# One part of a depthwise convolution as matmuls with diagonal weights on TensorE

## Chip, cores and metric

The kernel runs on one core of one Trainium2 chip. The metric is the device time of one execution in microseconds (us), as the median of several runs.

## What is computed

One block of a hybrid network: x is 1024 tokens by 1024 channels. After a modulated RMS norm the input is projected (`w_in`) for two branches: a gated depthwise convolution of 512 channels with 31 taps, and an RWKV-7 recurrence of eight heads of 64 channels. Both are joined, projected (`w_out`) and added; a second modulated norm and a gated feed-forward network with a 3-tap convolution follow. The change touches the first branch alone:

```python
def causal_dwconv(x, w, b):
    K, C = w.shape
    y = lax.conv_general_dilated(x, w[:, None, :].astype(x.dtype), window_strides=(1,),
                                 padding=[(K - 1, 0)], dimension_numbers=('NWC', 'WIO', 'NWC'),
                                 feature_group_count=C)
    return y + b

def token_mix(h, w_in, conv_dw_w, conv_dw_b, ...):
    p = h @ w_in
    p_conv, p_rw = p[..., :2 * CONV_WIDTH], p[..., 2 * CONV_WIDTH:]
    u, u_gate = jnp.split(p_conv, 2, axis=-1)
    u = u * jax.nn.sigmoid(u_gate)
    u = causal_dwconv(u, conv_dw_w, conv_dw_b)
    u = jax.nn.silu((layer_norm(u, LN_EPS) * conv_ln_g + conv_ln_b).astype(h.dtype))
    ...
    return jnp.concatenate([u, y], axis=-1) @ w_out
```

## The kernel before

Everything lies channels by tokens: 128 channels on the partitions, 512 tokens (a **half**) along them; half 0 is tokens 0 to 511. The recurrence goes in four **units** of 256 tokens, 0 and 1 in half 0, 2 and 3 in half 1.

Matmuls of the projections keep nearly full precision with three products: each weight tile of 128x512 (four blocks of 128x128) is loaded by SP's queue, cast to a high part `wh` by ScalarE (L140) and reduced to a low part `wl` by GpSimd (POOL, L142); the inputs are split the same way. L158 multiplies `wh` by the high input, L159 `wh` by the low one, L160 `wl` by the high one, all into one PSUM bank.

Names: `p_r10` is the projection of r for half 1 and the first group of heads, `p_k11` that of k for the second group, `p_ug1_0` and `p_u1_0` the gate and the value of the convolution's part 0 of half 1. A unit has pair blocks (`s`, L621, split by VectorE (DVE) at L623 to L625), an inverse of a triangular matrix on DVE (`inverse`, L663 to L683) whose input `ab` and output `dd` pass through DRAM, a merge (`pt`, L701) and a chain of steps (`ch`, `y`). `bo` (L609) is a unit's bonus term, a full-precision 128x512 matmul of r with a constant; `bo20` and `bo21` are those of unit 2. `cm0` (L427) is the matmul that takes the mean over the channels of half 0's convolution, `o000` the first tile of the output projection of half 0, `up00` the first tile of its up-projection; `hl_o00` to `hl_o03` are the low parts of o's first inputs (L454), the convolution's results.

The convolution of a half (`conv`) has four parts of 128 channels. Parts 0 to 2 run on DVE (`vector`, L396): 31 operations each, a tap at a time, into a PSUM bank. Part 3 (`scalar`) runs on ScalarE, one multiplication a tap (L400, L403), and POOL, which adds each product to the sum (L404). The function is a generator: every `shifted` (a projection of half 1 mixed with its shifted self), `glu` and `up_tile` takes one step of it, `next(filler[0], None)`. For half 0 a step is eight DVE taps, with a tap of part 3 beside every third:

```python
while n < 3 * KC:
    for j in range(taps):
        i = next(v, None)
        ...
        if n % 3 == 0:
            i = next(s, None)
            ...
        n += 1
    yield
```

So half 0's convolution is strewn over half 1's input projections. The Tile scheduler orders the instructions of each engine by priorities; blocks under `first()` (recurrence, `conv_norm`, the splits of the convolution's results) and under `high_priority` (the output projection) come ahead of others once ready, and `keep_in_program_order` pins the first tap of a step.

Of the kernel before, what the change touches and what calls it, by code (L numbers as in the profile page):

```python
# [7 lines left out]
F32 = mybir.dt.float32  # L8
# [59 lines left out]
def build(nc, tc, I, O):  # L68
# [306 lines left out]
    def conv(half, accs, taps):  # L375
# [12 lines left out]

        def vector():

            for ct in range(3):
                u, acc = load(ct), bank(f"cv{half}_{ct}", "v")
                yield V.tensor_scalar(acc, u[:, 0:HT], cw(ct, 0), col("conv_b", ct), ALU.mult, ALU.add)
                for k in range(1, KC):
                    o = accs[ct] if k == KC - 1 else acc
                    yield V.scalar_tensor_tensor(o, u[:, k:k + HT], cw(ct, k), acc, ALU.mult, ALU.add)  # L396

        def scalar():
            u, acc = load(3), accs[3]
            yield S.activation(acc, u[:, 0:HT], AF.Identity, scale=cw(3, 0), bias=col("conv_b", 3))  # L400
            for k in range(1, KC):
                t = slot(cv, "ctmp", f"{half}_{k}", bufs=2)
                i = S.activation(t, u[:, k:k + HT], AF.Identity, scale=cw(3, k), bias=ZERO)  # L403
                G.tensor_tensor(acc, acc, t, ALU.add)  # L404
                yield i

        v, s = vector(), scalar()
        n = 0
# [12 lines left out]
    def conv_norm(accs, half, b):  # L421
# [7 lines left out]
        for ct in range(4):  # L429
            V.tensor_tensor(accs[ct], accs[ct], mean, ALU.add)  # L430
            sq = s2 if ct == 0 else slot(cv, "ctmp", f"sq{half}_{ct}", bufs=2)
            S.activation(sq, accs[ct], AF.Square, bias=ZERO)
            if ct:
                G.tensor_tensor(s2, s2, sq, ALU.add)
        rb = bcast(rstd(s2, f"cv{half}", ones, 1, 1.0 / CW, EPS_LN, tag="c", b=b), f"cv{half}", 1, b=b)
        for ct in range(4):
            V.tensor_tensor(accs[ct], accs[ct], rb, ALU.mult)
            t = slot(cv, "ctmp", f"th{half}_{ct}", bufs=2)
            S.activation(t, accs[ct], AF.Tanh, scale=col("ln_g", ct), bias=col("ln_b", ct))
# [67 lines left out]
    def v_tiles(half):  # L507

        new = lambda q, g: rw.tile([P, 2, QT], F32, name=f"v{2 * half + q}{g}", tag="v", bufs=5)
        t = {(q, g): new(q, g) for q, g in ((0, 0), (0, 1), (1, 0), (1, 1))}  # L510
# [26 lines left out]
    def group_back(q, g):  # L537
        kvr = []
        for x in range(3):
            t = rw.tile([P, 2, QT], F32, name=f"{'kvr'[x]}{q}{g}", tag="kvr"[x], bufs=(3, 5, 3)[x])  # L540
            nc.sync.dma_start(t, kvd[g][x][:, q % 2])
            kvr.append({q % 2: t})
# [481 lines left out]
    def unit(q, kvrs, la, before=None):  # L1024
# [4 lines left out]
        if before:  # L1029
            with first():  # L1030
# [8 lines left out]
    ctags = ("ctmp", "cu", "ctmp", "cu3", "cacc0")  # L1039
    spare = ada_rest(range(3), lambda i, n: slot(cv, ctags[i % 5], n, 30 + HT if ctags[i % 5][:2] == "cu" else HT,  # L1040
                                                 2 if ctags[i % 5] == "ctmp" else 1)[:, :HT],
# [95 lines left out]
def layout(inp):  # L1137
# [21 lines left out]
    for p in range(4):  # L1159
        cols += [12 + p, 16 + p, 8 + p]  # L1160
    win = mt(w_in[:, :22 * P])[cols]
    winl = w_in[:, 22 * P:].reshape(8, P, 1, 32).transpose(1, 0, 2, 3).repeat(3, 2).reshape(P, 768)
    ada = a["ada_w"][0]
    am = ada.reshape(8, P, 6, 2, HT).transpose(2, 3, 0, 1, 4)
# [25 lines left out]
```

## Time and profile before

| | us |
|---|---|
| median of 3 runs (1476.76 to 1481.39) | 1479.4 |
| the profiled execution | 1478.2 |
| its span, first to last instruction | 1476.4 |
| mean granted TensorE clock, share of full speed | 0.964 |

The profile is of one execution. TensorE is PE, its weight loads PEld, VectorE DVE, ScalarE ACT, GpSimd POOL, SyncE SP. A clock of 1.00 in a window is the higher of TensorE's two levels (2.4 GHz); below that, it spent part of the window at 1.2 GHz. Half 0's convolution lies between 235 and 379 us, the recurrence of unit 2 between 390 and 515, half 0's output projection between 460 and 553, and the first up-projection starts at 584.7 us.

### The profile page before, as it was taken

How to read it: one execution, taken by the hardware profiler on the slowest of the kernel's cores; microseconds unless marked ns; L12 is line 12 of the kernel's file. 1: busy time of each engine (PE TensorE's matmuls, PEld its weight loads, DVE VectorE, ACT ScalarE, POOL GpSimd, SP SyncE). 2: the span in 40 equal slices, each digit the busy share in tenths (PEclk: the TensorE clock that was granted, in tenths of full speed). 3: DMA queues.
4: the chain of work that ended last, by engine and by line, in shares of the span. 5: the costliest groups of instructions: out<-in, count | busy, mean ns of one | idle time of the engine just before them, and what ended most of it. 6: DMA issues, size and time to landing. Idle time of an engine off the chain costs nothing.

```text
span 1476.4 us, 23402 instructions
## 1 busy us (share of the span) xinstructions
PE 1379.4 (93%) x8412; PEld 1115.5 (76%) x8412; DVE 915.0 (62%) x1427; ACT 682.0 (46%) x1234; POOL 783.0 (53%) x716
## 2 busy tenths in 40 slices
PE   3999989999899997999999999999998999999995
PEld 2787867777577885777788787777887888888884
DVE  7667669899765466888779965562027555551102
ACT  5445354365553465444555454644233444443221
POOL 2545654588653354555666654457446555454443
PEclk9999989999899896999999999999999999999997
DMA  9394572345323753235337345883335323233332
GB/s 358 118 351 139 171 202 93 116 121 152 97 79 106 184 161 106 66 90 150 96 107 217 122 147 188 295 285 91 94 96 183 110 94 99 95 98 93 92 98 75
DMA packets 168484, 208.02 MB, mean 141 GB/s; under 512 B 64112, under 2 KB 79088, under 8 KB 168368
## 3 DMA queue, kind: packets, MB, share of 16 engines
q1 hardware_dynamic: 167792, 205.48, 44.5%
q8 instruction: 66, 1.08, 0.3%
q10 hardware_dynamic: 576, 1.05, 0.2%
q14 instruction: 50, 0.41, 0.1%
HBM read 172.39 MB, written 34.08 MB: 140 GB/s over the span
## 4 chain that ended last, share of the span: by engine, by line
PE 67%; DVE 18%; DMA 6%; issue 3%; ACT 2%; SPq 2%; POOL 1%; DVEq 0%; POOLq 0%; ACTq 0%
PE up L158 9%; PE up L159 9%; PE up L160 9%; PE d L160 5%; PE d L158 5%; PE d L159 5%; DVE cv L396 2%; PE o L160 1%; PE o L158 1%; PE o L159 1%; DVE rkp L599 1%; DVE bk L601 1%; DVE t_dx L678 1%; PE s L621 1%; PE hn L708 1%
## 5 line engine op out<-in xcount | busy, mean ns | idle before, releaser
L142 POOL TENSOR_TENSOR wl_up<-w_up,wh_up 128x512 fp32r<-128x512 f32 x176 | 236.6, 1346 | 190.3 <-ACT wh_up L140 173.3
L140 ACT CAST wh_up<-w_up 128x512 fp32r<-128x512 f32 x176 | 108.9, 619 | 198.2 <-PE up L159 121.3
L142 POOL TENSOR_TENSOR wl_dn<-w_dn,wh_dn 128x512 fp32r<-128x512 f32 x96 | 116.8, 1220 | 118.6 <-ACT wh_dn L140 117.0
L158 PE MATMUL up<-hh_o,wh_up 128*128 128x512 f32 x352 | 141.3, 402 | 4.3 <-DVE q_za L949 4.2
L158 PE MATMUL up<-hh_f,wh_up 128*128 128x512 f32 x352 | 138.0, 392 | 4.1 <-DVE q_za L949 4.1
L160 PE MATMUL up<-hh_o,wl_up 128*128 128x512 f32 x352 | 141.7, 403 | 0.0
L159 PE MATMUL up<-hl_o,wh_up 128*128 128x512 f32 x352 | 140.7, 400 | 0.0
L160 PE MATMUL d<-ah,wl_dn 128*128 128x512 f32 x352 | 139.4, 397 | 1.0 <-POOL wl_dn L142 1.0
L159 PE MATMUL d<-al,wh_dn 128*128 128x512 f32 x352 | 139.4, 396 | 0.0
L158 PE MATMUL d<-ah,wh_dn 128*128 128x512 f32 x352 | 139.3, 396 | 0.0
L160 PE MATMUL up<-hh_f,wl_up 128*128 128x512 f32 x352 | 137.5, 391 | 0.0
L159 PE MATMUL up<-hl_f,wh_up 128*128 128x512 f32 x352 | 137.4, 390 | 0.0
L396 DVE SCALAR_TENSOR_TENSOR cv<-cu,pv,cv 128x512 f32<-128x512 f32 x174 | 130.2, 748 | 2.3
L994 DVE TENSOR_SCALAR mo_f<-d,mod 128x512 f32<-128x512 f32 x16 | 12.0, 749 | 180.9 <-ACT q_sqd L993 169.6
L140 ACT CAST wh_dn<-w_dn 128x512 fp32r<-128x512 f32 x96 | 56.0, 584 | 146.6 <-PE d L159 121.5
L944 DVE SCALAR_TENSOR_TENSOR q_za<-up,pv,q_za 128x510 f32<-128x510 f32 x88 | 65.6, 745 | 88.4 <-ACT q_za L942 88.2
L404 POOL TENSOR_TENSOR cacc<-cacc,ctmp 128x512 f32<-128x512 f32 x60 | 79.0, 1316 | 48.8 <-ACT ctmp L403 38.5
L158 PEld LDWEIGHTS up<-hh_o,wh_up 128*128 128x128 f32 x352 | 67.4, 192 | 19.3 <-DVE q_za L949 4.8
L158 PEld LDWEIGHTS up<-hh_f,wh_up 128*128 128x128 f32 x352 | 66.5, 189 | 18.6 <-ACT wh_up L140 4.5
L160 PEld LDWEIGHTS d<-ah,wl_dn 128*128 128x128 f32 x352 | 66.1, 188 | 17.6 <-POOL wl_dn L142 1.9
L160 PEld LDWEIGHTS up<-hh_o,wl_up 128*128 128x128 f32 x352 | 67.4, 191 | 14.9 <-issue 0.5
L158 PEld LDWEIGHTS d<-ah,wh_dn 128*128 128x128 f32 x352 | 66.1, 188 | 16.2 <-ACT wh_dn L140 0.4
(449 smaller groups left out, 3466.8 us busy)
## 6 DMA issues: line engine op xcount, KB each, us to landing
w_up<-w_up SPq DMA_DIRECT2D x176, 256.0 KB, 2.6
w_dn<-w_down SPq DMA_DIRECT2D x80, 256.0 KB, 2.7
w_o<-w_out SPq DMA_DIRECT2D x48, 256.0 KB, 3.4
aw_ada<-ada SPq DMA_DIRECT2D x32, 256.0 KB, 5.4
act<-q_za SPq DMA_DIRECT2D x22, 256.0 KB, 2.1
ax<-act SPq DMA_DIRECT2D x22, 256.0 KB, 4.6
ctmp_adb<-ada SPq DMA_DIRECT2D x20, 256.0 KB, 4.9
cu_adb<-ada SPq DMA_DIRECT2D x19, 256.0 KB, 4.5
```

The costliest lines, as they stand in the source:

```text
L140: S.copy(hi, w)
L142: e.tensor_tensor(lo, w, hi.bitcast(F32), ALU.subtract)
L158: TE.matmul(ps, wh[:, o], xh, start=k == 0, stop=False)
L159: TE.matmul(ps, wh[:, o], xl, start=False, stop=False)
L160: TE.matmul(ps, wl[:, o], xh, start=False, stop=k == K - 1)
L396: yield V.scalar_tensor_tensor(o, u[:, k:k + HT], cw(ct, k), acc, ALU.mult, ALU.add)
L404: G.tensor_tensor(acc, acc, t, ALU.add)
L599: V.tensor_tensor(pic(rkp[x][:, :, 1 + hh, :])[r], part(kkn, x)[r], half(eprev, x)[r], ALU.mult)
L601: V.tensor_tensor(bk[r, :, 1 - hh, :], v3(k)[r], v3(einv)[r], ALU.mult)
L621: TE.matmul(pss[hh][:, d], bk[r, ci(x, d)], rkp[x][r, d, 0:2 + hh:1 + hh, :], start=True, stop=True)
L678: V.tensor_tensor(t[:, i], u.unsqueeze(2).broadcast_to([P, n, n, n]), v.rearrange("p s c -> p c s").unsqueeze(1).broadcast_to([P, n, n, n] ...
L944: V.scalar_tensor_tensor(a[:, 2:], ps[:, 0:HT - 2], fw(0), a[:, 2:], ALU.mult, ALU.add)
```

## The change

Part 3 of half 0's convolution becomes matmuls. The host lays out a new input `cdiag`: for each part and tap a 128x128 matrix with the taps of the 128 channels on its diagonal. A matmul of such a matrix with the part's input, shifted by k tokens, is tap k for all channels; 31 of them accumulate in one PSUM bank. Input and weights are split in high and low parts and multiplied in three products, as in the projections: 93 matmuls of 128x512. The weights come as eight tiles of four taps (the last of three) through the same `weight` as others. One ScalarE operation with the bias brings the sum to SBUF. All of it is issued at one place, the filler's fourth step (n == 3), that is behind the `shifted` of r10; the DVE parts go on at eight taps a step. Half 1's convolution is unchanged.

The tiles `ctmp` grow from 512 to 542 columns to hold the split input, and the v tiles of the recurrence go from five buffers to four.

```diff
+        def tensor(cts):
+
+            for ct in cts:
+                u, ps = load(ct), bank(f"cd{half}_{ct}", "m")
+                uh = slot(cv, "ctmp", f"uh{half}_{ct}", 30 + HT, 2, F32R)
+                ul = slot(cv, "ctmp", f"ul{half}_{ct}", 30 + HT, 2, F32R)
+                S.copy(uh, u)
+                G.tensor_tensor(ul, u, uh.bitcast(F32), ALU.subtract)
+                for k0 in range(0, KC, 4):
+                    kn = min(4, KC - k0)
+                    wh, wl = weight(I["cdiag"][ct][:, k0 * P:(k0 + kn) * P], f"cd{half}_{ct}_{k0}", kn * P)
+                    for k in range(k0, k0 + kn):
+                        o, t = slice((k - k0) * P, (k - k0 + 1) * P), slice(k, k + HT)
+                        TE.matmul(ps, wh[:, o], uh[:, t], start=k == 0, stop=False)
+                        TE.matmul(ps, wh[:, o], ul[:, t], start=False, stop=False)
+                        TE.matmul(ps, wl[:, o], uh[:, t], start=False, stop=k == KC - 1)
+                    if k0 + kn == KC:
+                        S.activation(accs[ct], ps, AF.Identity, scale=0.5, bias=col("conv_b", ct))
+                    yield
...
-                t = slot(cv, "ctmp", f"{half}_{k}", bufs=2)
+                t = slot(cv, "ctmp", f"{half}_{k}", 30 + HT, 2)[:, :HT]
...
-        v, s = vector(), scalar()
+        if half == 0:
+
+            v = vector(range(3))
+            for n in range(100):
+                for j in range(taps):
+                    i = next(v, None)
+                    if i is not None and j == 0:
+                        tc.keep_in_program_order(i)
+                if n in (3, 8):
+                    for _ in tensor([c for c in range(3, 4) if (c == 3) == (n == 3)]):
+                        pass
+                if n > 8 and i is None:
+                    return
+                yield
+
+        v, s = vector(range(3)), scalar()
...
-        new = lambda q, g: rw.tile([P, 2, QT], F32, name=f"v{2 * half + q}{g}", tag="v", bufs=5)
+        new = lambda q, g: rw.tile([P, 2, QT], F32, name=f"v{2 * half + q}{g}", tag="v", bufs=4)
...
-            t = rw.tile([P, 2, QT], F32, name=f"{'kvr'[x]}{q}{g}", tag="kvr"[x], bufs=(3, 5, 3)[x])
+            t = rw.tile([P, 2, QT], F32, name=f"{'kvr'[x]}{q}{g}", tag="kvr"[x], bufs=(3, 4, 3)[x])
...
+    cw = a["conv_dw_w"][0].reshape(KC, 4, P)
+    cdiag = np.zeros((4, P, KC, P), np.float32)
+    cdiag[:, np.arange(P), :, np.arange(P)] = cw.transpose(2, 1, 0)
+    cdiag = cdiag.reshape(4, P, KC * P)
```

The order of the instructions moves with it. The line numbers of the new kernel are 35 higher from L427 on. PE's order behind the last matmuls of r10, in the kernel before:

```order
L159 MATMUL p_r10_3452<-hl_1_7_3265,wh_r10_4_3473 128x512
L160 MATMUL p_r10_3452<-hh_1_7_3262,wl_r10_4_3475 128x512
L158 MATMUL p_k11_3517<-hh_1_0_3227,wh_k11_0_3520 128x512
L159 MATMUL p_k11_3517<-hl_1_0_3230,wh_k11_0_3520 128x512
L160 MATMUL p_k11_3517<-hh_1_0_3227,wl_k11_0_3522 128x512
L158 MATMUL p_k11_3517<-hh_1_1_3232,wh_k11_0_3520 128x512
L159 MATMUL p_k11_3517<-hl_1_1_3235,wh_k11_0_3520 128x512
```

and in the changed one (`cd0_3` is the new bank, `ctmp_uh0_3` and `ctmp_ul0_3` the split input):

```order
L159 MATMUL p_r10_3426<-hl_1_7_3265,wh_r10_4_3447 128x512
L160 MATMUL p_r10_3426<-hh_1_7_3262,wl_r10_4_3449 128x512
L402 MATMUL cd0_3_3484<-ctmp_uh0_3_3485,wh_cd0_3_0_3491 128x512
L403 MATMUL cd0_3_3484<-ctmp_ul0_3_3486,wh_cd0_3_0_3491 128x512
L404 MATMUL cd0_3_3484<-ctmp_uh0_3_3485,wl_cd0_3_0_3493 128x512
L402 MATMUL cd0_3_3484<-ctmp_uh0_3_3485,wh_cd0_3_0_3491 128x512
L403 MATMUL cd0_3_3484<-ctmp_ul0_3_3486,wh_cd0_3_0_3491 128x512
```

The 93 new matmuls stand where the projection of k for the second group of heads stood; that and all later projections of half 1 follow them.

PE's order around the bonus of unit 2 (`bo20`), before:

```order
L159 MATMUL p_ug1_1_4760<-hl_1_7_3265,wh_ug1_1_4_4781 128x512
L160 MATMUL p_ug1_1_4760<-hh_1_7_3262,wl_ug1_1_4_4783 128x512
L609 MATMUL bo20_4113<-r20_4033,cst_78 128x512
L763 MATMUL y1_0_2948<-uv1_0_2930,bkt010_2483 64x64
L160 MATMUL p_u1_1_4799<-hh_1_0_3227,wl_u1_1_0_4804 128x512
L158 MATMUL p_u1_1_4799<-hh_1_1_3232,wh_u1_1_0_4802 128x512
L159 MATMUL p_u1_1_4799<-hl_1_1_3235,wh_u1_1_0_4802 128x512
```

and now:

```order
L160 MATMUL p_ug1_0_4694<-hh_1_7_3262,wl_ug1_0_4_4717 128x512
L798 MATMUL y1_0_2948<-uv1_0_2930,bkt010_2483 64x64 x4
L798 MATMUL y1_0_2948<-uv1_0_2930,bkt011_2609 64x64 x4
L644 MATMUL bo20_4169<-r20_4089,cst_78 128x512
L462 MATMUL cm0_5057<-cu_s0_5053,cst_78 128x512
L158 MATMUL p_u1_0_4733<-hh_1_0_3227,wh_u1_0_0_4736 128x512
L159 MATMUL p_u1_0_4733<-hl_1_0_3230,wh_u1_0_0_4736 128x512
L160 MATMUL p_u1_0_4733<-hh_1_0_3227,wl_u1_0_0_4738 128x512
```

The projection beside `bo20` is that of part 0 now (of part 1 before), the `y1_0` matmuls stand ahead of `bo20`, and `cm0` directly behind it.

DVE's order where the low parts of the output projection's first inputs are made, before (`t_dt2_0` opens unit 2's inverse; the rows left out are of the same inputs, an input's split and a tap of other work):

```order
L625 TENSOR_TENSOR rkp121_4220<-s21_11_4263,cst_78 64x4x64
L454 TENSOR_TENSOR hl_o02_5059<-cacc2_0_2_3750,hh_o02_5058 128x512
...
L454 TENSOR_TENSOR hl_o03_5061<-cacc3_0_3_3318,hh_o03_5060 128x512
L371 SCALAR_TENSOR_TENSOR q_u1_3_4994<-q_sg1_3_4955,p_u1_3_4957 128x512
...
L454 TENSOR_TENSOR hl_o04_5063<-q_mi04_5086,hh_o04_5062 128x256
...
L454 TENSOR_TENSOR hl_o05_5065<-q_mi05_5090,hh_o05_5064 128x256
L454 TENSOR_TENSOR hl_o06_5067<-q_mi06_5094,hh_o06_5066 128x256
L454 TENSOR_TENSOR hl_o07_5069<-q_mi07_5098,hh_o07_5068 128x256
L663 TENSOR_TENSOR t_dt2_0_4302<-ab2_4294,dm2_4299 128x12
L665 TENSOR_TENSOR dm2_4299<-dm2_4299,t_dt2_0_4302 128x4x3
```

and now:

```order
L660 TENSOR_TENSOR rkp121_4276<-s21_11_4319,cst_78 64x4x64
L800 TENSOR_TENSOR zv1_3_3145<-y1_3_3149,zv1_3_3145 64x4x64 x2
L371 SCALAR_TENSOR_TENSOR q_u1_2_4971<-q_sg1_2_4932,p_u1_2_4934 128x512
L698 TENSOR_TENSOR t_dt2_0_4358<-ab2_4350,dm2_4355 128x12
L700 TENSOR_TENSOR dm2_4355<-dm2_4355,t_dt2_0_4358 128x4x3
...
L713 TENSOR_TENSOR t_dx2_80_4375<-ab2_4350,dm2_4355 128x512
...
L718 TENSOR_REDUCE dm2_4355<-t_dx2_81_4378 128x8x8
L719 COPY dm2_4355<-dm2_4355 128x16x16
L489 TENSOR_TENSOR hl_o00_5111<-cacc0_0_0_3312,hh_o00_5110 128x512
...
L489 TENSOR_TENSOR hl_o03_5117<-cacc3_0_3_3483,hh_o03_5116 128x512
...
L371 SCALAR_TENSOR_TENSOR q_u1_3_5050<-q_sg1_3_5011,p_u1_3_5013 128x512
```

The inverse of unit 2 stands ahead of the four splits now, where it stood behind them.

## Rows read from the trace of the kernel before

**Rows 1.** The page: busy time, share of the span and instructions of each engine.

```profile
PE 1379.4 (93%) x8412; PEld 1115.5 (76%) x8412; DVE 915.0 (62%) x1427; ACT 682.0 (46%) x1234; POOL 783.0 (53%) x716
```

**Rows 2.** Windows: from:to, length, busy of PE, PEld, DVE, ACT, POOL (instructions); clock, DMA.

```profile
250.00:288.00 38.00, 37.95 (x297) 30.51 (x297) 33.37 (x53) 15.00 (x29) 20.41 (x23) 1.00 0.42 128
288.00:345.00 57.00, 54.21 (x374) 41.05 (x372) 55.38 (x93) 33.93 (x53) 45.93 (x44) 1.00 0.43 118
345.00:404.00 59.00, 49.96 (x479) 37.57 (x479) 49.49 (x71) 31.51 (x58) 42.59 (x33) 0.85 0.39 116
404.00:460.00 56.00, 52.67 (x425) 39.85 (x423) 33.77 (x66) 25.84 (x50) 24.97 (x22) 0.92 0.28 88
460.00:508.00 48.00, 45.19 (x359) 41.87 (x357) 26.59 (x49) 22.10 (x46) 20.87 (x18) 0.89 0.59 153
...
553.00:585.00 32.00, 22.48 (x210) 17.52 (x210) 22.01 (x52) 16.32 (x37) 11.99 (x14) 0.72 0.33 107
1360.00:1400.00 40.00, 40.00 (x173) 32.22 (x172) 4.04 (x6) 11.27 (x19) 18.64 (x16) 1.00 0.35 96
```

**Rows 3.** The chain that ended last, 255 to 262 and 300 to 315: start, us, what.

```profile
256.25 0.23 PE p_k L158
...
261.09 0.61 PE y L773 x16
...
301.48 1.10 POOL cacc L404
...
305.32 0.81 POOL cacc L404
...
312.38 1.30 POOL cacc L404
```

**Rows 4.** Part 3's operations, 290 to 400 us, and L400: ns min/median/max, first and last start.

```profile
L403 ACT ACTIVATE ctmp<-cu,small,pv x30: 799/814/819, 296.1 to 376.1; 128x512 f32<-128x512 f32 x30
L404 POOL TENSOR_TENSOR cacc<-cacc,ctmp x30: 1259/1292/1614, 297.0 to 377.4; 128x512 f32<-128x512 f32 x30
...
L400 ACT ACTIVATE cacc<-cu,pv x2: 815/816/816, 295.4 to 604.7; 128x512 f32<-128x512 f32 x2
```

**Rows 5.** Weight tiles: L140, L142, loads (KB, us to landing), a page group.

```profile
L140 ACT CAST wh_k<-w_k x14: 602/619/623, 39.9 to 301.2; 128x512 fp32r<-128x512 f32 x14
...
L142 POOL TENSOR_TENSOR wl_k<-w_k,wh_k x14: 1262/1290/1733, 45.5 to 302.7; 128x512 fp32r<-128x512 f32 x14
...
w_k<-w_in SPq DMA_DIRECT2D x4, 256.0 KB, 3.0
...
v<-vd SPq DMA_DIRECT2D x1, 256.0 KB, 2.7
...
L160 PE MATMUL d<-ah,wl_dn 128*128 128x512 f32 x352 | 139.4, 397 | 1.0 <-POOL wl_dn L142 1.0
```

**Rows 6.** The chain that ended last around bo20.

```profile
400.18 1.66 DVE bk L604
...
402.90 1.96 PE bo L609 x2
```

**Rows 7.** DVE: the taps (whole span), bk at 385 to 404 and 560 to 580 us.

```profile
L396 DVE SCALAR_TENSOR_TENSOR cv<-cu,pv,cv x174: 732/748/762, 235.8 to 837.9; 128x512 f32<-128x512 f32 x174
...
L601 DVE TENSOR_TENSOR bk<-k,einv_cs x2: 1690/1729/1768, 395.0 to 396.8; 64x512 f32<-64x512 f32 x2
...
L601 DVE TENSOR_TENSOR bk<-k,einv_cs x2: 675/682/689, 569.9 to 570.6; 64x512 f32<-64x512 f32 x2
```

**Rows 8.** The first output projection's and the first up-projection's matmuls (455 to 475, 580 to 592).

```profile
L158 PE MATMUL o<-hh_o,wh_o x13: 274/282/385, 460.0 to 474.7; 128*128 128x256 f32 x13
...
L158 PE MATMUL up<-hh_o,wh_up x6: 389/628/774, 584.7 to 591.4; 128*128 128x512 f32 x6
```

**Rows 9.** Unit 2: the s matmuls (400 to 470 us) and the inverse's reductions (470 to 490).

```profile
L621 PE MATMUL s<-rkp,bk x64: 272/272/373, 417.4 to 462.4; 64*128 64x128 f32 x64
...
L683 DVE TENSOR_REDUCE dm<-t_dx x4: 286/486/686, 479.1 to 483.6; 128x32 f32<-128x128 f32 x2, 128x64 f32<-128x512 f32 x2
```

More of the change, by code (lines that the diff above doesn't have):

```diff
@@ L387, in load, with vector @@
             return u
-        def vector():
-            for ct in range(3):
+        def tensor(cts):
[16 more added lines that the diff above has]
+                    yield
+        def vector(cts):
+            for ct in cts:
                 u, acc = load(ct), bank(f"cv{half}_{ct}", "v")
@@ L430, in conv_norm @@
             V.tensor_tensor(accs[ct], accs[ct], mean, ALU.add)
-            sq = s2 if ct == 0 else slot(cv, "ctmp", f"sq{half}_{ct}", bufs=2)
+            sq = s2 if ct == 0 else slot(cv, "ctmp", f"sq{half}_{ct}", 30 + HT, 2)[:, :HT]
             S.activation(sq, accs[ct], AF.Square, bias=ZERO)
@@ L437, in conv_norm @@
             V.tensor_tensor(accs[ct], accs[ct], rb, ALU.mult)
-            t = slot(cv, "ctmp", f"th{half}_{ct}", bufs=2)
+            t = slot(cv, "ctmp", f"th{half}_{ct}", 30 + HT, 2)[:, :HT]
             S.activation(t, accs[ct], AF.Tanh, scale=col("ln_g", ct), bias=col("ln_b", ct))
@@ L1039, in build @@
     ctags = ("ctmp", "cu", "ctmp", "cu3", "cacc0")
-    spare = ada_rest(range(3), lambda i, n: slot(cv, ctags[i % 5], n, 30 + HT if ctags[i % 5][:2] == "cu" else HT,
+    spare = ada_rest(range(3), lambda i, n: slot(cv, ctags[i % 5], n, HT if ctags[i % 5] == "cacc0" else 30 + HT,
                                                  2 if ctags[i % 5] == "ctmp" else 1)[:, :HT],
@@ L1091, in build @@
             split_in(accs[k], *h[k])
-    ms = [slot(cv, t, f"m{m}", 30 + HT if t[:2] == "cu" else HT, 2 if t == "ctmp" else 1)[:, :HT] for m, t in enumerate(mtags)]
+    ms = [slot(cv, t, f"m{m}", HT if t[:4] == "cacc" else 30 + HT, 2 if t == "ctmp" else 1)[:, :HT] for m, t in enumerate(mtags)]
     with tc.high_priority(offset=500000):
@@ L1170, in layout @@
         "xT": c(a["x"][0].T.reshape(8, P, 2, HT).transpose(2, 0, 1, 3)),
-        "xR": c(a["x"][0][HT:].reshape(4, P, 2, HT)), "ada1": c(ada1), "ada2": c(ada2), "w_in": c(win), "w_inl": c(winl),
+        "cdiag": cdiag, "xR": c(a["x"][0][HT:].reshape(4, P, 2, HT)), "ada1": c(ada1), "ada2": c(ada2), "w_in": c(win), "w_inl": c(winl),
         "w_out": c(mt(a["w_out"][0])), "w_up": c(mt(a["w_up"][0])),
```

## The prediction

> **What bounds the kernel now.** Read the page's busy shares first. TensorE (PE) is busy for 1379.4 of the span's 1476.4 us, the other engines for 62% or less [rows 1]. That average says that added PE work is paid in full. It is not enough: the change touches only the stretch from 250 to 585 us. From the first up-projection tile on (584.7 us) the order of every engine is the same in both kernels, and so are the weights. So read the table of windows next [rows 2]. From 250 to 288 us PE is busy 37.95 of 38 us at full clock, and the chain of waits that ended last is there a row of matmuls 0.23 us apart [rows 3]: PE is the bound. From 288 to 345 us VectorE (DVE) is the fuller engine, 55.38 of 57 us, and the chain leaves PE: from 300 to 315 us it runs through GpSimd (POOL), five of its pieces being the very additions that the change removes [rows 3]. From 345 to 404 us PE does 49.96 us in 59 and the granted clock is 0.85: part of the time it ran at the lower of its two levels. From 404 to 460 us PE is nearly full again (52.67 of 56, clock 0.92), to 508 us too (45.19 of 48, clock 0.89), and the last 32 us before the up-projection are loose: 22.48 us busy, clock 0.72. So there is slack on PE in this stretch, but it lies behind the place where the new matmuls stand, and reaches the end only if work can slide into it.
>
> **The change part by part.**
>
> Added on PE: 31 taps times three products are 93 matmuls of 128x512. In a dense stretch 173 such matmuls take 40.00 us [rows 2], 0.231 us each; the chain shows 0.23 [rows 3]. I take 0.233, so **+21.7 us** of PE work. They stand where PE is full (behind the projection r10).
>
> Removed: on ScalarE one 0.816 and 30 multiplications of 0.814 us, 25.2 us; on POOL 30 additions of 1.292 us, 38.8 us [rows 4]. They ran from 296 to 379 us. On the chain I find only the five additions between 300 and 315 us, 1.10 to 1.30 us long with the shorter ones at 0.81 and 0.86, together 5.35 us [rows 3].
>
> Added beside PE: eight weight tiles for the diagonals. The nearest rows are the tiles of w_k: a load of 256 KB that lands in 3.0 us, a ScalarE cast of 0.619 us and a POOL subtraction of 1.29 us [rows 5]; eight of them and the split of u (one cast, one subtraction) are 5.6 us of ScalarE and 11.6 us of POOL. A tile feeds twelve matmuls, 2.8 us of PE, as an ordinary projection tile of the same size does, so its POOL work hides behind PE as theirs does: 0. The bounds are 0 and, if the first tile comes late, one load, cast and subtraction, 4.9 us; nothing can be gained by loading more. SP's queue carries eight more loads; those of k11 behind them are needed 21.7 us later too. Smaller buffers (v tiles five to four) hold back a load only if the fifth was ahead of need; I see no PE wait on a v tile, so 0, with one reload of 2.7 us [rows 5] as the bound.
>
> Moved: the order holds 27 more 128x512 matmuls between r10 and the matmul bo20 (first and second excerpt, PE), not 93. The 93 came in and 66 of the in-projection went behind bo20. That is 27 x 0.233 = 6.3 us, less one full-precision 128x512 matmul (cm0) that went behind it too (0.98 us, half of the bo pair [rows 6]), plus eight small ones: **+5.9 us ahead of bo20**. Here PE isn't the bound: bo20 waited for DVE, the last wait of a chain of DVE pieces that ends at 402.90 [rows 6]. DVE has the same number of instructions, and the work ahead of bo20's last input is about 6 us less in the new order, since taps and statistics of the convolution went behind. With the 5.35 us on POOL this says bo20 could come 5 us earlier; with PE's added work it could come 6 us later. I take **the old place, 403 us**, between -6 and +6.
>
> Would DVE itself be faster without POOL's 39 us? The tap operations, its main load, aren't: 732 to 762 ns over 174 of them, with POOL full or empty [rows 7]. Operations with two inputs in SBUF do stretch: 1.73 us at 395 us where the same shape takes 0.68 at 570 [rows 7]. But POOL at 395 us is busy with other work than the removed additions, which ended at 378.7 us [rows 4], so I count nothing.
>
> The Trainium skill has a rule on this ("SBUF — State Buffer", section "SBUF: two separate sides"): a VectorE operation with two SBUF inputs and a GpSimd operation that reads SBUF exclude each other for a whole instruction. The trace agrees on the stretch (1.73 against 0.68 us); by the rule, four such operations ahead of bo20 freed of POOL would give 4 x 1.0 us back, and the sum would end 4 us lower.
>
> From bo20 to the first output projection o000: 57.1 us in before (402.9 to 460.0 [rows 6, 8]). The new order has 181 matmuls of 128x512 there against 101: 80 x 0.233 = 18.6 us; cm0, 0.98 us; and 24 more 64-wide and 16 more 128-wide ones, for which I put 4 us (each lies between 0.04 us, the y piece of the chain [rows 3], and 0.27, an s matmul [rows 9]): **+24 us**. What it can fill: the old 56 us hold 3.3 us of idle PE and, at clock 0.92, 4.5 us lost to the lower level [rows 2]. With the projections lying dense I take both as gone: **-7.8 us**. o000 starts at 402.9 + 57.1 + 24 - 7.8 = 476 us. A second route: DVE now has unit 2's inverse ahead of the splits that o000 reads (third excerpt). In before the last s matmul ran at 462.4 and the inverse's last reduction began at 483.6 [rows 9], 21.2 us; behind the last s matmul the new order has 17 us of PE work ahead of o000, so PE waits some 5 us there. The 3 us are cm0's: it stands directly behind bo20 now and waits for two DVE operations of 1.66 us that moved behind bo20's inputs and for one sum behind them, of about as much, less bo20's own 1.96 us [rows 6]. o000 comes at 403 + 49.4 (the PE work from bo20 to the last s) + 3 + 21.9 (the 21.2 and one split) = 477 to 478. The two agree within 2 us; I keep the sum.
>
> From o000 to the up-projection: 124.6 us in before [rows 8]. Since more was finished ahead, the new order holds 14 fewer 128x512, 32 fewer 64-wide and 16 fewer 128-wide matmuls: 3.3 + 2.5 + 2.2 = **-8 us**. The loose end (553 to 585 us) hangs on a chain through ScalarE, DVE and POOL that the change leaves alone: 0.
>
> Sum: 0 (bo20) + 24 - 7.8 - 8 = **+8.2 us**. The profiled execution took 1478.2 us (span 1476.4), 1.2 below the median of 1479.4; 1478.2 + 8.2 gives **1486 us**.
>
> **The rivals.**
>
> A, nothing is absorbed: PE is the bound throughout and each added matmul counts, 1478.2 + 21.7 = 1500 us. For it: 93% busy, and the place behind r10. Against: from 288 to 404 us PE idles 11.8 us and loses 9 us to the clock [rows 2].
>
> B, level: bo20 comes 6 us early by the removed additions and the shorter DVE list, the rest as in the sum: 8.2 - 6 = +2, about 1480 us, between 1475 and 1483.
>
> C, faster (the other side): the chain through DVE and POOL sets the pace from 288 to 404 us, and the new matmuls only fill PE beneath it. Price: -9 us at bo20 (5.35 from POOL, 4 from the stretched DVE operations); +24 - 7.8 behind; -8 in the output projections; and the clock of the remaining loose stretches (0.89 and 0.72) rises, which gives back up to 5 + 9 us [rows 2], of which half: -9 + 24 - 7.8 - 8 - 7 = -8, 1470 us. It decides from the point at which bo20 comes before 396 us and the granted clock from 345 on is near 1.
>
> D, the weights come late: each of eight tiles stalls the new matmuls because POOL is in the middle of another tile. A wait of 1.29 us for each is 10 us more: 1496 us. Against: the same pattern feeds every in-projection, and in the page's group of 352 projection matmuls PE waits 1.0 us in all for POOL's tiles [rows 5].
>
> **How the numbers follow.** About 0.3% (4.4 us) is what a measurement of this kernel can tell from no change. The forecast (1483 to 1493): 0.45. A: 0.10, D: 0.05. B: 0.17. C: 0.23. The forecast's lower edge and B share the band within 0.3%: same 0.20; faster is C and a little of B, 0.25; slower 0.55. The range leaves out half of A and the lower third of C: 1471 to 1499.
>
> **What would show it.** PE from 265 to 295 us: 93 matmuls in one piece, 0.23 us apart (if gaps of over 0.5 us stand between groups of twelve, D). bo20 at 397 to 409 us (earlier, C). From bo20 to o000 some 73 us, clock above 0.95 (below, A). o000 at 474 to 478 us with a wait of about 5 us for DVE's splits. o000 to the first up tile 117 us. The forecast is wrong if the stretch before bo20 shrinks by more than 6 us, or if the loose 32 us before the up-projection tighten.

## The result: 0.9% slower

The changed kernel took 1490.1 us (median of 8 runs, 1486.4 to 1501.3), the kernel before 1478.9 (8 runs, 1475.6 to 1482.9): a ratio of 1.0091, 95% interval 1.0068 to 1.0115, that is +13.4 us, between 10 and 17. The forecast was 1486 in a range of 1471 to 1499. The profiled execution took 1490.6 us with a span of 1488.7, 12.4 us more than that of before.

First the page of the changed kernel, its busy shares (as in [rows 1]):

```profile
PE 1393.4 (94%) x8505; PEld 1130.4 (76%) x8505; DVE 907.4 (61%) x1427; ACT 665.7 (45%) x1213; POOL 752.5 (51%) x695
```

TensorE (PE) is busy 14 us longer for 93 more instructions, ScalarE (ACT) 16 and GpSimd (POOL) 31 us shorter. VectorE (DVE) has the same 1427 instructions and 7.6 us less to do. Next the windows that answer [rows 2] (from:to, length, busy of PE, PEld, DVE, ACT and POOL with their counts, clock, DMA share, GB/s):

```profile
250.00:288.00 38.00, 37.76 (x297) 29.73 (x297) 30.55 (x49) 12.79 (x28) 19.08 (x20) 1.00 0.23 69
288.00:345.00 57.00, 56.05 (x437) 44.01 (x436) 39.88 (x75) 19.86 (x34) 26.16 (x30) 0.97 0.49 131
345.00:404.00 59.00, 50.30 (x467) 37.85 (x466) 56.34 (x89) 23.89 (x46) 21.91 (x20) 0.97 0.46 150
404.00:460.00 56.00, 53.94 (x438) 41.79 (x438) 38.56 (x66) 28.26 (x54) 30.39 (x26) 0.94 0.29 86
460.00:508.00 48.00, 43.66 (x380) 38.16 (x377) 26.24 (x51) 19.91 (x41) 18.67 (x16) 0.93 0.60 152
```

From 288 to 404 us PE does 374 + 479 = 853 instructions in before and 904 now, and the clock of 345 to 404 us rose from 0.85 to 0.97: here added work was taken in. DVE's load moved back, from 288 to 345 us to the next window. The start times of the steps of the sum, from the tiles (ns min/median/max, first and last start):

```profile
L402 PE MATMUL cd<-ctmp_uh,wh_cd x31: 387/395/498, 249.6 to 283.5; 128*128 128x512 f32 x31
...
L644 PE MATMUL bo<-r,cst x2: 677/852/1027, 397.7 to 398.2; 128*128 128x512 f32 x2
...
L158 PE MATMUL o<-hh_o,wh_o x19: 279/283/580, 479.0 to 499.9; 128*128 128x256 f32 x19
...
L158 PE MATMUL up<-hh_o,wh_up x10: 387/391/774, 598.1 to 609.5; 128*128 128x512 f32 x10
```

| step | before | forecast | changed |
|---|---|---|---|
| start of bo20 | 402.9 | 403 (397 to 409) | 397.7 |
| bo20 to the first output projection o000 | 57.1 | 73.3 | 81.3 |
| o000 to the first up-projection up00 | 124.7 | 116.6 | 119.1 |
| up00 to the end of the execution | 893.5 | 893.5 | 892.5 |

So bo20 came 5.2 us early, and the stretch behind it cost 24.2 us, 8 more than the forecast's 16.2. What PE waited for from bo20 to the last tile of half 0's output projection, from the table of waits (us in total, times, longest), 397 to 480 us and 480 to 563 us (the first row is the wait ahead of bo20 itself):

```profile
PE bo L644 <- DVE r L642: 3.1, 1, 3.1
PE s L656 <- DVE bk L636: 1.9, 2, 1.0
PE cm L462 <- DVE cu_s L460: 0.4, 1, 0.4
...
PE pt L736 <- DMA dd<-sd: 4.3, 2, 2.5
```

The 3.3 us of idle time and the time lost to the lower clock were both to go; there are still 2.5 us of idle time in this stretch (81.3 less 78.8 busy), and the clock is 0.94 where it was to be 1.

### The profile page after: what moved, and what is told of

Same layout as the page of the kernel before. It is cut to its first block, busy times and chain, and to the rows that moved or that the text cites. A ratio compares the mean times of both kernels' runs of the same rounds, so it can differ in the third digit from the quotient of the medians.

```text
span 1488.7 us, 23568 instructions
## 1 busy us (share of the span) xinstructions
PE 1393.4 (94%) x8505; PEld 1130.4 (76%) x8505; DVE 907.4 (61%) x1427; ACT 665.7 (45%) x1213; POOL 752.5 (51%) x695
## 4 chain that ended last, share of the span: by engine, by line
PE 66%; DVE 19%; DMA 7%; issue 3%; ACT 2%; SPq 1%; POOL 1%; DVEq 0%; POOLq 0%; ACTq 0%
PE up L159 9%; PE up L158 9%; PE up L160 9%; PE d L160 5%; PE d L159 5%; PE d L158 5%; DVE cv L416 3%; PE o L158 2%; PE o L160 2%; PE o L159 2%; DVE rkp L634 1%; PE s L656 1%; DVE bk L636 1%; PE hn L743 1%; DVE t_dx L713 1%
## 5 line engine op out<-in xcount | busy, mean ns | idle before, releaser
L142 POOL TENSOR_TENSOR wl_up<-w_up,wh_up 128x512 fp32r<-128x512 f32 x176 | 236.6, 1346 | 197.9 <-ACT wh_up L140 179.0
L140 ACT CAST wh_up<-w_up 128x512 fp32r<-128x512 f32 x176 | 108.8, 619 | 197.5 <-PE up L159 115.8
L142 POOL TENSOR_TENSOR wl_dn<-w_dn,wh_dn 128x512 fp32r<-128x512 f32 x96 | 116.3, 1214 | 118.7 <-ACT wh_dn L140 114.9
L140 ACT CAST wh_dn<-w_dn 128x512 fp32r<-128x512 f32 x96 | 56.0, 584 | 148.8 <-PE d L159 126.5
L158 PEld LDWEIGHTS up<-hh_o,wh_up 128*128 128x128 f32 x352 | 67.3, 191 | 19.5 <-DVE q_za L984 4.8
L142 POOL TENSOR_TENSOR wl_o<-w_o,wh_o 128x512 fp32r<-128x512 f32 x32 | 42.5, 1332 | 74.8 <-ACT wh_o L140 74.7
L159 PEld LDWEIGHTS d<-al,wh_dn 128*128 128x128 f32 x352 | 66.1, 188 | 15.9
```

The lines of the kernel that those rows point to most:

```text
L140: S.copy(hi, w)
L142: e.tensor_tensor(lo, w, hi.bitcast(F32), ALU.subtract)
L158: TE.matmul(ps, wh[:, o], xh, start=k == 0, stop=False)
L159: TE.matmul(ps, wh[:, o], xl, start=False, stop=False)
```

## The experiments

Times are differences to the kernel before on the same chip, from the ratio of the runs, with its 95% interval. The starts are those of the traces, one execution of each kernel, up to 7 us off the kernel's median (additions_out 1470.4 against 1463.8). Kernels with one order on PE differ by some 3 us in the stretch from bo20 to o000: 72.9 us in add_only and 75.6 in add_only_v4, 81.3 in the changed kernel and 78.8 in one_tile; less than that is not read from a single trace. s20 is the first pair block of unit 2, the recurrence's next step behind bo20.

| kernel | time against before | bo20 | s20 | o000 | up00 |
|---|---|---|---|---|---|
| before | | 402.9 | 417.4 | 460.0 | 584.7 |
| changed | +13.4 (+10, +17) | 397.7 | 411.3 | 479.0 | 598.1 |
| remove_only | -21.3 (-25, -17) | 388.0 | 396.4 | 442.5 | 558.9 |
| add_only | +7.7 (+4, +11) | 399.8 | 404.3 | 472.7 | 590.1 |
| both_no_tiles | +15.2 (+12, +18) | 396.7 | 410.9 | 478.2 | 598.0 |
| one_tile | +11.7 (+8, +15) | 396.1 | 410.2 | 474.9 | 591.1 |
| add_only_v4 | +8.6 (+6, +11) | 399.5 | 405.6 | 475.1 | 592.5 |
| additions_out | -15.2 (-19, -11) | 398.2 | 409.3 | 436.0 | 573.7 |
| products_out | -5.9 (-9, -3) | 404.4 | 416.4 | 444.0 | 577.4 |
| later_n8 | +10.5 (+7, +14) | 396.1 | 410.3 | 473.1 | 592.2 |
| later_n6 | -0.1 (-3, +2) | 403.6 | 404.8 | 473.8 | 585.4 |
| one_product | -3.7 (-7, -1) | 394.2 | 407.2 | 461.5 | 577.6 |
| lean_31 | +2.4 (0, +5) | 399.7 | 412.7 | 467.0 | 583.2 |
| one_product_n2 | +12.4 (+8, +17) | 396.4 | 408.5 | 467.4 | 589.3 |

### The two halves, apart and together

Removal alone: in the kernel before, part 3 of half 0 keeps its first tap.

```diff
-            for k in range(1, KC):
+            for k in range(1, 1 if half == 0 else KC):
                 t = slot(cv, "ctmp", f"{half}_{k}", bufs=2)
```

> The kernel before without the work that the change takes from ScalarE and GpSimd: of part 3 of half 0's convolution only the first tap is computed, 30 multiplications and 30 additions are left out (the values of that part are not the convolution's). Nothing is added on TensorE. The theory (the added matmuls cost what they take from bo20 on, and bo20 itself comes early because the additions on GpSimd are gone): bo20 at 397 to 399 us instead of 402.9, the rest as before, time 4 to 6 us below the kernel before. Rival R (bo20 came early because VectorE's list was reordered, the additions lay off the path): bo20 at 402 to 404 us, time within 2 us of before.

Addition alone: 93 matmuls on the input's high part, at the same place of the filler.

```diff
         while n < 3 * KC:
+            if half == 0 and n == 3 * taps:
+                ps, (xh, xl) = bank("cd0_3", "m"), h[0]
+                for k in range(93):
+                    TE.matmul(ps, xh[:, 0:P], xh, start=k == 0, stop=k == 92)
+                S.copy(cp.tile([P, 1], F32, name="cdx"), ps[:, 0:1])
             for j in range(taps):
```

> The kernel before, with its ScalarE and GpSimd taps kept, and 93 more matmuls of 128x512 of the same type behind r10, on tiles that are in SBUF already, into a bank that nothing uses. So the matmuls alone, without weight tiles, loads or removal; PE's order is nearly that of the changed kernel. The theory: +17 to +19 us against before (the changed kernel's +12.3 and the 5 us that the removal gave), with bo20 at 402 to 408 us. Rival R (the reordered lists made bo20 early): the same +12 us as the changed kernel and bo20 at 398 us. Rival W (part of the changed kernel's loss is the weight tiles): under +10 us.

Both diffs in one kernel:

> The two halves together: the 30 multiplications and additions of part 3 left out (as in remove_only, so part 3's values are not the convolution's), and 93 matmuls on tiles in SBUF (as in add_only). No weight tiles, no split of u. The orders of PE and VectorE are those of the changed kernel. Theory W (the eight weight tiles are what the changed kernel pays beyond the two halves): the halves add up, -20.4 + 7.5 = -13 us against before, 1464 us. Theory S (the halves don't add up, since what the removal frees is time in which TensorE now has work; tiles cost nothing): as the changed kernel, +10 to +14 us, 1487 to 1491 us.

All three went against a part of what I held. The removal is worth 21 us, not 5; the 93 matmuls cost 8 us, not 18; and together they cost 15, where the sum of the two would be a gain of 14. Without a weight tile, a load or a split, both_no_tiles is as slow as the changed kernel, whose order on PE it has but for one place of three matmuls. So theory S stands: the loss comes from how the two meet. One thing these runs don't separate: whoever takes work out moves the order too. In remove_only s20 follows bo20 after 8.4 us, in before after 14.5, and add_only's order is another than that of both_no_tiles; so the 21 us are those of the removal together with the order that came with it. Windows of remove_only up to bo20, from there to o000, and to up00:

```profile
248.00:388.00 140.00, 133.04 (x1160) 104.08 (x1158) 129.43 (x215) 58.99 (x111) 66.91 (x69) 0.98 0.44 131
388.00:442.50 54.50, 54.50 (x455) 42.35 (x455) 37.95 (x75) 26.14 (x51) 27.66 (x26) 1.00 0.30 96
442.50:558.90 116.40, 102.92 (x960) 90.88 (x958) 77.12 (x151) 65.53 (x146) 48.76 (x46) 0.92 0.54 158
```

and of the kernel before over the same steps:

```profile
250.00:402.90 152.90, 141.02 (x1148) 108.75 (x1147) 138.07 (x215) 79.58 (x137) 108.93 (x99) 0.94 0.42 121
402.90:460.00 57.10, 53.77 (x425) 40.23 (x425) 33.95 (x67) 26.70 (x51) 24.97 (x22) 0.91 0.28 87
460.00:584.70 124.70, 110.03 (x997) 97.25 (x996) 75.30 (x158) 66.64 (x147) 51.89 (x49) 0.89 0.52 148
```

Up to bo20 DVE has the same 215 instructions in both and does them in 129.4 us instead of 138.1. PE's clock rises in all three stretches, in the second to 1.00 with no idle time at all. In add_only the first stretch gains too, and the second is as dense (its windows from bo20 to o000 and to up00):

```profile
399.80:472.70 72.90, 71.95 (x544) 56.18 (x544) 56.13 (x103) 40.28 (x76) 38.34 (x33) 1.00 0.36 109
472.70:590.10 117.40, 100.87 (x880) 89.00 (x881) 62.93 (x131) 61.89 (x138) 46.52 (x43) 0.86 0.52 154
```

against the changed kernel:

```profile
397.70:479.00 81.30, 78.83 (x587) 60.21 (x588) 58.02 (x105) 39.73 (x75) 39.95 (x34) 0.94 0.34 97
479.00:598.10 119.10, 103.15 (x887) 93.17 (x887) 62.23 (x130) 61.78 (x137) 44.48 (x43) 0.83 0.53 152
```

An estimate shows how the two meet. Counting PE's work in the order at full clock (0.233 us for each 128x512 product, the small ones at their spacing in dense runs), bo20 has some 316.6 us of it ahead in before, 314.6 in remove_only, 325.3 in add_only and 322.5 in the changed kernel. Its start lies 86, 73, 74 and 75 us behind that. (What the small ones are priced at moves the level of such a count, but hardly the differences.) Each half takes the same 11 to 13 us of loss out of the stretch before bo20, and the second one finds nothing left to take. That is about a third of what the sum misses: up00 comes 25.8 us earlier by the removal alone and 5.4 later by the addition alone, but 13.3 later by both, 34 us from the sum. Of these, 12 are there at bo20; the others arise behind it.

### Tiles, loads and buffers

One weight tile instead of eight:

```diff
-                    wh, wl = weight(I["cdiag"][ct][:, k0 * P:(k0 + kn) * P], f"cd{half}_{ct}_{k0}", kn * P)
+                    if k0 == 0:
+                        wh, wl = weight(I["cdiag"][ct][:, k0 * P:(k0 + kn) * P], f"cd{half}_{ct}_{k0}", kn * P)
```

> The changed kernel with one weight tile in place of eight: the first tile's four taps serve for all 31 (part 3's values are not the convolution's); the split of u, the 93 matmuls and the orders of all engines but for the seven tiles are the changed kernel's. Theory W: 5 us or more below the changed kernel, close to both_no_tiles. Theory S: within 3 us of the changed kernel.

add_only with the changed kernel's two lines for the v tiles:

```diff
-        new = lambda q, g: rw.tile([P, 2, QT], F32, name=f"v{2 * half + q}{g}", tag="v", bufs=5)
+        new = lambda q, g: rw.tile([P, 2, QT], F32, name=f"v{2 * half + q}{g}", tag="v", bufs=4)
...
-            t = rw.tile([P, 2, QT], F32, name=f"{'kvr'[x]}{q}{g}", tag="kvr"[x], bufs=(3, 5, 3)[x])
+            t = rw.tile([P, 2, QT], F32, name=f"{'kvr'[x]}{q}{g}", tag="kvr"[x], bufs=(3, 4, 3)[x])
```

> add_only with four v buffers in place of five, as the changed kernel has; the order of TensorE is the same. If the fifth buffer was needed: 3 to 6 us above add_only, and a wait on a load of v in front of it. If not (the prediction's 0): within 2 us of add_only, +7.5 us against before.

Neither is told apart from its parent: 11.7 us against 13.4, and 8.6 against 7.7, both inside the intervals. The prediction's two zeros hold.

### Which of the removed engines

The kernel before without the additions, then without the multiplications of part 3 (the additions then take u itself):

```diff
-                G.tensor_tensor(acc, acc, t, ALU.add)
+                if half:
+                    G.tensor_tensor(acc, acc, t, ALU.add)
```

> The kernel before with the 30 additions of part 3 on GpSimd left out (its values are not the convolution's) and the 30 multiplications on ScalarE kept. Nothing on TensorE. Theory G (what the removal frees is GpSimd: its queue, and VectorE's operations with two inputs in SBUF, which were 8 us shorter up to bo20 in remove_only): most of remove_only's -20 us, 1456 to 1464 us. Rival (ScalarE's 25 us stood in front of other casts): within 5 us of the kernel before.

```diff
-                i = S.activation(t, u[:, k:k + HT], AF.Identity, scale=cw(3, k), bias=ZERO)
-                G.tensor_tensor(acc, acc, t, ALU.add)
+                if half:
+                    i = S.activation(t, u[:, k:k + HT], AF.Identity, scale=cw(3, k), bias=ZERO)
+                    G.tensor_tensor(acc, acc, t, ALU.add)
+                else:
+                    i = G.tensor_tensor(acc, acc, u[:, k:k + HT], ALU.add)
```

> The counterpart: the 30 multiplications on ScalarE left out, the 30 additions on GpSimd kept (they add the unscaled input, so part 3's values are not the convolution's). Its order on TensorE is that of additions_out within 3 us of work. Theory G: within 5 us of the kernel before. Rival: 1456 to 1464 us.

Theory G holds in the main: the additions are worth 15 us and the multiplications 6, together the 21 of remove_only. The second number is a little outside the "within 5 us", though its interval reaches into it. These kernels have orders of their own too (301 and 316 matmuls from bo20 to o000, where before has 425), so either number holds for the removal with its order. By a count as above, bo20 lies some 13 us nearer to the work ahead of it in additions_out than in before, and some 4 us in products_out.

Part of the 15 is DVE's two-input operations. The same operations of the convolution's sum and of unit 1's inverse up to bo20 (line, shapes, count, busy us, mean ns, idle before), in before:

```profile
L424 DVE TENSOR_TENSOR cu_s<-cu_s,cacc 128x512 f32<-128x512 f32 x1 | 1.6, 1639 | 0.0
...
L665 DVE TENSOR_TENSOR dm<-dm,t_dt 128x16 f32<-128x16 f32 x1 | 1.3, 1324 | 0.0
L663 DVE TENSOR_TENSOR t_dt<-ab,dm 128x16 f32<-128x16 f32 x1 | 1.2, 1211 | 0.0
```

and in remove_only:

```profile
L424 DVE TENSOR_TENSOR cu_s<-cu_s,cacc 128x512 f32<-128x512 f32 x1 | 0.7, 693 | 0.0
...
L665 DVE TENSOR_TENSOR dm<-dm,t_dt 128x16 f32<-128x16 f32 x1 | 0.2, 180 | 0.0
L663 DVE TENSOR_TENSOR t_dt<-ab,dm 128x16 f32<-128x16 f32 x1 | 0.2, 178 | 0.0
```

The two short ones beside what POOL did at that time, in before (start, us):

```profile
322.45 1.21 DVE L663 TENSOR_TENSOR t_dt<-ab,dm 128x16 f32<-128x16 f32 x1
323.69 1.32 DVE L665 TENSOR_TENSOR dm<-dm,t_dt 128x16 f32<-128x16 f32 x1
...
322.32 1.31 POOL L142 TENSOR_TENSOR wl_gd<-w_gd,wh_gd 128x512 fp32r<-128x512 f32 x1
...
323.68 1.30 POOL L404 TENSOR_TENSOR cacc<-cacc,ctmp 128x512 f32<-128x512 f32 x1
```

Each takes as long as the POOL operation beside it: one lies under an addition of part 3, the other under a weight tile's subtraction that queued among the additions. These two and L424 alone are 3.1 us. The additions' being there isn't enough: in products_out, which keeps them, the same two take 0.17 and 0.18 us.

### The place in the order

The changed kernel with `n == 8` and with `n == 6` in place of 3:

```diff
-                if n in (3, 8):
-                    for _ in tensor([c for c in range(3, 4) if (c == 3) == (n == 3)]):
+                if n == 8:
+                    for _ in tensor([3]):
```

> The changed kernel with the 93 matmuls issued at the filler's step 8 instead of step 3, that is five projections later: in PE's order they start after 233 us of PE work instead of 195, where PE has idle time and ran at the lower clock in the kernel before (345 to 404 us). If the place counts (the slack of 345 to 404 us was out of reach at step 3): 4 to 9 us below the changed kernel. The theory (the same PE work has to be done ahead of the output projection from either place): within 3 us of the changed kernel.

> The changed kernel with the 93 matmuls issued at step 6. Unit 2's first pair block s20 stands 1 us of TensorE work behind bo20 there, in the changed kernel 11 us (the projection p_u1_0 lies between). If the order behind bo20 costs what add_only and the changed kernel differ by (8 us at up00; s20 came 4.5 and 13.6 us after bo20): s20 at or before 405 us, o000 at or before 474 us, 4 to 8 us below the changed kernel. If the sum of TensorE's work alone counts: within 3 us of the changed kernel.

Step 8 did nothing clear to the time (10.5 against 13.4, the intervals overlap), as the theory had it. Step 6 took the whole loss back, with the same matmuls, tiles and removal: more than the 4 to 8 us expected, and far outside the theory's 3. s20 is 1.2 us behind bo20 there, 13.6 in the changed kernel. From bo20 to o000 and from there to up00:

```profile
403.60:473.80 70.20, 68.23 (x525) 54.27 (x525) 49.26 (x98) 35.61 (x66) 38.27 (x32) 1.00 0.40 117
473.80:585.40 111.60, 97.95 (x875) 86.09 (x875) 60.44 (x128) 60.76 (x135) 41.97 (x41) 0.88 0.53 158
```

Clock 1.00 where the changed kernel has 0.94, and 0.88 where it has 0.83. Of the 12.7 us by which up00 comes earlier than in the changed kernel, 5.2 lie ahead of o000 and 7.5 behind it. later_n8 over the same two steps:

```profile
396.10:473.10 77.00, 74.99 (x603) 58.33 (x603) 51.05 (x101) 38.15 (x72) 38.79 (x35) 1.00 0.39 111
473.10:592.20 119.10, 99.00 (x878) 88.34 (x874) 64.71 (x137) 63.79 (x139) 46.30 (x43) 0.89 0.49 149
```

It reaches o000 as early as later_n6 and at clock 1.00, although s20 lies 14.2 us behind its bo20; its loss is all behind o000, 119.1 us against 111.6.

The waits of later_n6 from 474 to 552 us hold none of pt (merge of unit 2) on the dd loads:

```profile
PE o L160 <- DVE wl_o L142: 1.4, 2, 0.7
PE o L158 <- ACT hh_o L488: 0.6, 1, 0.6
PE c_f L192 <- DVE q_sqf L892: 0.2, 1, 0.2
```

### Fewer matmuls

One product a tap at step 3 (31 matmuls of 93):

```diff
                         TE.matmul(ps, wh[:, o], uh[:, t], start=k == 0, stop=k == KC - 1)
-                        TE.matmul(ps, wh[:, o], ul[:, t], start=False, stop=False)
-                        TE.matmul(ps, wl[:, o], uh[:, t], start=False, stop=k == KC - 1)
```

> The changed kernel with one product a tap instead of three: 31 matmuls (the low parts of taps and input are left out of part 3), all else the same. The theory (each added matmul costs its 0.233 us): 62 x 0.233 = 14.4 us less than the changed kernel, 1474 to 1477 us, that is 2 to 5 us below the kernel before. Rival I (what costs is the new place of unit 2's inverse ahead of the splits that the output projection reads, on VectorE, which this kernel has as well): at most half of it back, 1481 to 1486 us.

For lean_31 also:

```diff
-                ul = slot(cv, "ctmp", f"ul{half}_{ct}", 30 + HT, 2, F32R)
...
-                G.tensor_tensor(ul, u, uh.bitcast(F32), ALU.subtract)
...
-                    wh, wl = weight(I["cdiag"][ct][:, k0 * P:(k0 + kn) * P], f"cd{half}_{ct}_{k0}", kn * P)
+                    w = slot(wp, "w", f"cd{half}_{ct}_{k0}", kn * P, 3)
+                    nc.sync.dma_start(w, I["cdiag"][ct][:, k0 * P:(k0 + kn) * P])
+                    wh = slot(wp, "wh", f"cd{half}_{ct}_{k0}", kn * P, 3, F32R)
+                    S.copy(wh, w)
```

> A version that may beat both: one product a tap as in one_product (low parts left out), and so no split of u and no subtraction for the eight weight tiles: 31 matmuls of 128x512, eight loads, nine ScalarE casts, nothing on GpSimd. TensorE's work grows by 7.2 us. The theory: as one_product or up to 5 us less, 1467 to 1472 us, since GpSimd isn't what bounds it there. Theory W: 4 to 10 us below one_product, since half of a tile's cost is gone.

And one_product with `n == 2` for the step:

> A version that may beat both: one product a tap (31 matmuls, low parts of part 3 left out) at step 2 instead of 3; unit 2's blocks stand some 4 us earlier in TensorE's order than in one_product (s20 at 323 us of work against 327, its last block at 356 against 361). If the recurrence leads: 3 to 5 us below one_product, 1466 to 1470 us. If TensorE's work alone counts: as one_product, 1470 to 1474 us.

one_product met its number: 17 us below the changed kernel, where 62 matmuls are 14.4. But the other two show that this says little for "each matmul its 0.233 us". lean_31 has as many matmuls and less on POOL; it was expected level or up to 5 us faster, and is some 6 us slower, the intervals next to each other. Its bo20 comes 5.5 us later; its order on PE is another up to bo20 and the same from there to o000 (67.3 us in both). What in it costs the 5.5 us, these runs don't tell. And one_product_n2, with 31 matmuls, costs as much as the changed kernel with 93. There the matmuls come ahead of r10, and PE waits for pair blocks at 266 us. Its waits from 255 to 275 us, and its windows before and in that wait:

```profile
PE s L654 <- DVE rkp L658: 3.8, 2, 3.0
...
240.00:262.00 22.00, 22.00 (x213) 17.71 (x213) 20.22 (x29) 11.92 (x24) 17.54 (x15) 1.00 0.40 119
262.00:275.00 13.00, 9.20 (x44) 7.45 (x43) 12.50 (x23) 1.76 (x3) 1.96 (x3) 0.65 0.28 89
```

A wait of 3.8 us, and a granted clock of 0.65 in those 13 us. But one_product has that wait too, and the lower clock:

```profile
PE s L654 <- DVE rkp L658: 4.3, 1, 4.3
...
262.00:275.00 13.00, 8.97 (x46) 7.04 (x46) 10.44 (x18) 2.22 (x4) 4.88 (x4) 0.74 0.25 81
```

So it is not what sets the two apart. bo20 of one_product_n2 comes 2.2 us later than that of one_product, o000 5.9 and up00 11.7: most of the loss lies behind bo20. There PE waits for the dd loads of unit 2's merge, which it doesn't in one_product:

```profile
PE pt L734 <- DMA dd<-sd: 4.5, 1, 4.5
```

The rest of the 11.7 us stays open. No kernel here keeps all three products and is faster than the kernel before; one_product is, by 0.25% (0.05 to 0.45%), and leaves the low parts out.

## Why the forecast was right, and where its working was not

**The sign and the size.** +8.2 us was forecast for the profiled execution, 12.4 came. Two steps of the sum missed, in opposite directions: bo20 (0 taken, -5.2 found, inside the bounds of -6 and +6) and the stretch behind it (+16.2 taken, +24.2 found). From o000 to up00 -8 was taken and -5.6 found: the output projection gave the 8, but the loose end grew from 32.2 to 34.6 us. That the total is only 4.2 us off is in part luck, since the first two misses offset each other by 5 us.

**bo20.** The two effects that I set against each other were both there, but the removal was mis-sized. I priced it by the five additions that lie on the chain, 5.35 us [rows 3]; remove_only puts bo20 14.9 us earlier. An operation that holds up others appears on the chain under the names of those others: DVE's list became 8.6 us shorter with the same instructions, and PE's clock rose from 0.94 to 0.98. "I count nothing" for the stretched operations of DVE is the step that failed. It rested on the pair at 395 us, where other work of POOL was to blame, and left out those between 320 and 326 us, under the additions and the subtractions queued among them. That the tap operations don't stretch was right (750 ns in before, 749 in remove_only). bo20's own operations changed as well, in the changed kernel:

```profile
L636 DVE TENSOR_TENSOR bk<-k,einv_cs x2: 672/680/689, 393.4 to 394.1; 64x512 f32<-64x512 f32 x2
...
L639 DVE SCALAR_TENSOR_TENSOR bk<-a,einv_cs x2: 676/683/690, 397.5 to 398.2; 64x512 f32<-64x512 f32 x2
...
L642 DVE SCALAR_TENSOR_TENSOR r<-r,pv,k x2: 1392/1434/1476, 394.8 to 396.1; 128x256 f32<-128x256 f32 x2
```

The four bk operations take 0.68 us each where they took 1.73 and 1.66, the 4 us that the rule of the Trainium skill ("SBUF — State Buffer", section "SBUF: two separate sides") gave. But only two of them still stand ahead of bo20, and the two of r, which now run beside two weight subtractions of POOL (394.6 to 397.3 us), take 1.43 instead of 0.48 us each, 1.9 us lost again. So by the rows the gain at bo20's own operations depends on what POOL does at that moment, and the larger part of the 8.6 us of remove_only lies elsewhere.

**The 7.8 us behind bo20** are the term that failed: next to nothing of the idle time and of the loss to the clock was taken in. The work itself was sized right: 78.8 us busy at clock 0.94 are some 74 us at full clock (an estimate), and the sum had 73.3. The absorption could be had in other orders: add_only needs 72.9 us from bo20 to o000 and later_n6 70.2 (with fewer matmuls there), both at clock 1.00. The changed kernel needs 81.3. Its order has cm0 and the projection p_u1_0 between bo20 and s20. The chain of waits at bo20 (start, us, what):

```profile
394.77 2.79 DVE r L642 x2
...
398.89 0.70 DVE cu_s L460
...
399.64 1.22 PE cm L462
```

PE waits for r, then for the sum behind it, drops to the lower clock (0.94 over the stretch), and then does p_u1_0 while s20, the recurrence's next step, stands behind it. s20 starts 13.6 us after bo20; in later_n6 1.2. I had priced cm0's wait of 3 us in the second route, and let it go in the sum. cm0 itself, priced at half of bo20's pair of records, 0.98 us, is such a pair too and took 2.07. That route, through the last s and the inverse, gave 477 to 478 us for o000, and it came at 479.0; but that is luck. bo20 came 5.3 us ahead of the 403 that it starts from, and its 49.4 + 3 us from there to the last s (460.6) were 62.9. The wait at its end didn't come; from the last s to o000 PE has no idle time:

```profile
460.60:479.00 18.40, 18.40 (x130) 14.66 (x127) 13.00 (x28) 7.51 (x15) 9.56 (x8) 1.00 0.38 92
```

The inverse's last reduction began 15.4 us behind the last s, not 21.2. A wait stood further on: pt, 5.7 us behind o000, waited 4.3 us for the dd loads.

That the order and not the tiles makes the loss is shown by both_no_tiles (same order, same loss, no tiles) and by later_n6 (the same added and removed work, another order, no loss). What in the order does it isn't shown. s20's place alone doesn't: in later_n8 it lies as far behind bo20, and PE reaches o000 at clock 1.00. cm0 directly behind bo20 is what only the changed kernel, both_no_tiles and one_tile have, with clocks of 0.94, 0.93 and 0.97 up to o000; that fits, but no run moves it alone. And a good stretch up to o000 isn't enough: later_n8 has one, and loses behind o000.

**The rivals.** A (all 21.7 us paid) has the time wrong by 10 us in the changed kernel, and its rule fails: with the removal, the 93 matmuls end 15 us above before at step 3 and level with it at step 6; alone they cost 8; and 31 at step 2, removal included, end 12 above. B, level, is what later_n6 is. In the changed kernel B had bo20 right (5 of its 6 us), but not the rest. C's first half happened in part (bo20 early, though not before 396 us), its second didn't. D is out: no wait of cd on a tile shows, and one tile is not told apart from eight (11.7 against 13.4).

**What would show it.** The 93 matmuls were to lie in one piece between 265 and 295 us. They lie between 249.6 and 284.0, 0.23 us apart with small matmuls of the recurrence between them and no wait on a tile: right as far as D goes. bo20 at 397 to 409: right, at the edge (397.7). Some 73 us to o000 at a clock above 0.95: wrong, 81 at 0.94, the sign that was to speak for A, though what was lost was not the matmuls' price. "o000 at 474 to 478" with a wait of 5 us for the splits: 479.0, without it. 117 us from o000 to up00: 119.

## What to carry to other kernels

Work taken from a side engine is priced by what it holds up, not by its own pieces on the chain: leave it out and run once. Two changes that fill the same slack don't add up; a table of starts less the work ahead, step by step, shows when the slack is used up. And where TensorE works in program order, the place of added matmuls can count for more than their number: try a few places before judging the idea, and read in each trace which stretch the difference lies in.

## What was not expected of the hardware

VectorE operations of 128x16 elements took 1.2 to 1.3 us, as long as the GpSimd operation beside them (an addition or a weight tile's subtraction of 128x512, 1.3 us), and 0.18 us without one. TensorE's clock mostly went with short waits: 1.00 in one_product_n2 over 22 us without any, and 0.65 over the next 13 us, which hold a wait of 3.8 us. From bo20 to o000 it was 1.00 with 0 to 2.8 us of waits at bo20 and behind it (remove_only, add_only, later_n6, later_n8), and 0.94 with 5.4 us in the changed kernel. But add_only_v4, with the order of add_only and the same 2.8 us of waits, had 0.95: the waits alone don't settle it.
